# Seven-product FFN, first sweep: who rounds the weights, where raw weights land, and how the operands of the last token group are built

## Chip, core and metric

One core of a Trainium2 chip runs the whole program. The metric is the device time of one execution in microseconds (us); the median of three executions stands for a kernel.

## What is computed

The reference is a two-layer backbone of a latent generator, in fp32: 1024 latent tokens and 256 context tokens, model width 1024, hidden width 4096. Each layer has four mixers (bidirectional SSD, RG-LRU, global and windowed attention) and then the part that matters here, the MLP:

```python
h = modulate(rms_norm(x, g2), shift, scale)
x = x + gate * (square(relu(h @ w_ffn1)) @ w_ffn2)
```

Layer 0 computes this for latent and context tokens, layer 1 for the latent tokens alone, since only these are returned.

## The kernel before

Every fp32 operand of a matmul is split in two: a rounded part `h` (type fp32r) and the remainder `l = raw - h`. A product is then three matmuls, wh·hh, wh·hl and wl·hh (`mm3`, L141 to L143). For weights this is `wsplit`: for each of two halves a DMA of SyncE's queue brings 128x512 raw values, `split` (L242 to L249) rounds them into `wh` and subtracts into `wl`. The pools hold 3 tiles `wh`, 3 `wl`, 2 `raw`, and 8 work tiles `s` (128x512, made by `self.S`) that all helpers share.

The first matmul of the MLP multiplies 1024x1024 latent values (two groups of 512 tokens, g0 and g1) by `w_ffn1` with a seven-product scheme: in blocks of two by two, seven products of sums of blocks replace eight. Two of the products use the weights as they are and the token group g0 alone; they are done first, in `hidden_first` (L1259 to L1307), which runs while the normalised values of g1 are not there yet. The other five, in `hidden_rest`, need sums of operand blocks and sums of weight blocks.

- `hidden_first` steps over the 32 blocks `fc` of 128 hidden rows. For an even `fc`, `part` makes a product of 12 matmuls over the upper half of the contraction; ScalarE copies it out (`copy_a`, L130, b<-qk or b<-pm) and its DMA saves it (L1292); `second` adds the lower half on the same PSUM tile, and `squared` (L1253 to L1256) makes relu and square on ScalarE. In layer 0 every `fc` also has `context`, 24 matmuls over 256 tokens; in layer 1 only the 16 even `fc` are visited, and `second` of a step comes behind `part` of the next one.
- Woven in between (`weave` in `ffn`) stands the work on g1: squares and sums of the RMS norm (`norm_stats`, L412 to L422; its sum over partitions is the tiny matmul L418, its power -0.5 runs on GpSimd, L422), and then `quarter` (L1212 to L1250). This builds, for 4 pairs of rows (k, k+4), the sums of operand blocks on VectorE: `row` makes one modulated row (L136, which reads PSUM, and L1229), then come six subtractions and additions (L1238 to L1243) and five times a rounding CAST and a subtraction (L1248, L1249). It takes two values of k at a time: four rows first, then the 32 operations of both.
- `hidden_rest` begins with `weights(0)`, sums of raw blocks on VectorE (L1345 to L1348), rounding on ScalarE (L130, wh<-s) and subtractions on VectorE (L1351).

While `hidden_first` runs, `act_evicts` is set, and `split` rounds with `gpsimd.tensor_copy` (L246, a CAST); the subtraction is `gpsimd.tensor_sub` (L249). At all other times ScalarE does the rounding.

Each engine works off its own queue in order. The program's framework puts the instructions into these queues, by its own estimate of when each can start, and lets a tile be reused when its last reader is done. So an edit to one helper also shifts the order in which other instructions stand.

Of the kernel before, what the change touches and what calls it, by code (L numbers as in the profile page):

```python
# [13 lines left out]
P = 128  # L14
# [26 lines left out]
def f(ap):  # L41
    return ap.bitcast(F32)


def drain(g):
    for _ in g:
        pass
# [46 lines left out]
class Net:  # L94
# [147 lines left out]

    def split(self, h, l, raw):

        if self.act_evicts:
            self.nc.gpsimd.tensor_copy(h, raw)  # L246
        else:
            self.copy_a(h, raw)
        self.nc.gpsimd.tensor_sub(l, raw, f(h))  # L249


    act_evicts = False

    def wsplit(self, loads, n, new=None):

        if new:
            wl, wh = new(F32R)[:, :n], new(F32R)[:, :n]
        else:
            wl = self.W()[:, :n]
            wh = self.wp.tile([P, 4 * WU], F32R, tag="wh", name="wh", bufs=3)[:, :n]  # L260
        for i in range(2):
            raw = self.R(n // 2)
            for dst, src in loads(raw, i):
                self.nc.sync.dma_start(dst, src)
            c = slice(i * n // 2, (i + 1) * n // 2)
            self.split(wh[:, c], wl[:, c], raw)
        return wh, wl

    def wcols(self, w, c0):

        return self.wsplit(lambda r, i: [(r.rearrange("p (k c) -> p k c", k=4),
                                          w[512 * i:512 * i + 512, c0:c0 + P].rearrange("(k p) c -> p k c", p=P))], 1024)

    def wrows(self, w, r0, new=None):
        return self.wsplit(lambda r, i: [(r, w[r0:r0 + P, 512 * i:512 * i + 512])], 1024, new)
# [937 lines left out]
    def quarter(self, h, t, x, l, t0, rs):  # L1213

        nc = self.nc
        p = self.L[l]
        n = 512
        (hh, hl), (th, tl) = h, t  # L1220
        g0, g1 = G_LAT[0][0], G_LAT[1][0]
        rb = self.PS("pt")
        for j in range(4):
            nc.tensor.transpose(rb[:, j * P:(j + 1) * P], rs[:, j:j + 1].to_broadcast([P, P]), self.ident)

        def row(k):
            a = self.S(n)
            self.stt(a, x.at(k, t0, n), p["s"][1][:, k, 0:1], rb, ALU.mult, ALU.mult)
            nc.vector.tensor_scalar(a, a, p["mods"][:, 24 + k, 0:1], None, op0=ALU.add)  # L1229
            return a  # L1230
        for k2 in range(0, 4, 2):
            rows = [(k, row(k), row(k + 4)) for k in (k2, k2 + 1)]
            yield 2.0
            for k, b12, b22 in rows:
                t1, t2, t3, t4 = (self.S(n) for _ in range(4))
                b11h, b11l, b21h, b21l = (f(r.at(c, g0, n)) for c in (k, k + 4) for r in (hh, hl))
                sub, add = nc.vector.tensor_sub, nc.vector.tensor_add
                sub(t1, b12, b11h)  # L1238
                sub(t3, b22, b12)
                sub(t1, t1, b11l)  # L1240
                sub(t2, b22, t1)
                sub(t4, b21h, t2)
                add(t4, t4, b21l)  # L1243
                yield 2.0
                for raw, r, c, tg in ((t3, t, k + 4, g0), (b22, h, k + 4, g1), (t1, h, k, g1), (t2, t, k, g0),
                                      (t4, t, k, g1)):
                    oh, ol = r[0].at(c, tg, n), r[1].at(c, tg, n)
                    nc.vector.tensor_copy(oh, raw)  # L1248
                    sub(ol, raw, f(oh))  # L1249
                    yield 1.0  # L1250

    def squared(self, r, fc, t0, n, raw=None):

# [4 lines left out]
    def hidden_first(self, l, h, groups):  # L1258


        nc = self.nc
        hh, hl = h
        w1 = self.I["w_ffn1"][l]
        tags = ("pm", "qk", "qk")

        def part(ps, w, t0, n, ks):
            for k in ks:
                c = slice(k * P, k * P + P)
                self.mm3(ps, w[0][:, c], w[1][:, c], hh.at(k, t0, n), hl.at(k, t0, n), k == 0, k in (3, KD - 1), True)
                if k % 2:  # L1270
                    yield n * 2 * 3 * 216e-3 / 512

        def context(fc, w):
            t0, n = G_CTX
            ps = self.PS(self.pick(tags))[:, :n]
            yield from part(ps, w, t0, n, range(KD))
            self.squared(self.B(n), fc, t0, n, ps)

        def second(fc, w, ps):
            t0, n = G_LAT[0]  # L1280
            yield from part(ps, w, t0, n, range(4, KD))
            self.squared(self.B(), fc, t0, n, ps)
        last = None
        for fc in range(0, FFN // P, 1 if len(groups) == 3 else 2):
            w = self.next_weights()[0] if self.wq or self.ready else self.wcols(w1, fc * P)
            if fc % 2 == 0:
                t0, n = G_LAT[0]
                ps = self.PS(self.pick(tags))
                yield from part(ps, w, t0, n, range(4))
                r = self.B()  # L1290
                self.copy_a(r, ps)
                nc.scalar.dma_start(self.part[fc // 2], r)  # L1292

                if len(groups) == 3:
                    yield from context(fc, w)
                    yield from second(fc, w, ps)
                else:
                    if last:
                        yield from second(*last)
                    last = fc, w, ps  # L1300
            else:
                yield from context(fc, w)
        if last:
            yield from second(*last)

    def hidden_rest(self, l, h, t):
# [4 lines left out]
        nc = self.nc  # L1311
        (hh, hl), (th, tl) = h, t
        w1 = self.I["w_ffn1"][l]
        g0, g1 = G_LAT[0][0], G_LAT[1][0]
        n = 512
        NQ = FFN // 256

        def weights(q):
            if q:
                raws = []  # L1320
                for j in range(2):
                    r = self.U()[:, :1024].rearrange("p (k c) -> p k c", k=4)
                    nc.sync.dma_start(r, w1[512 * j:512 * j + 512, 256 * q:256 * q + 256].rearrange("(k p) c -> p k c", p=P))
                    raws.append(r)
                su = [self.U(), self.U()]
                sr = [su[i // 2][:, 512 * (i % 2):512 * (i % 2) + 512] for i in range(4)]
            else:

                raws = {}
                for i, j in ((0, 1), (1, 1), (0, 0), (1, 0)):  # L1330
                    r = (self.S() if j else self.R(512)).rearrange("p (k c) -> p k c", k=4)
                    nc.sync.dma_start(r, w1[512 * j:512 * j + 512, i * P:i * P + P].rearrange("(k p) c -> p k c", p=P))
                    raws[i, j] = r
                sr = [self.S() for _ in range(4)]

            def a(i, j):
                return raws[j][:, :, i * P:i * P + P] if q else raws[i, j]
            wl = [self.W()[:, :1024], self.W()[:, :1024]]
            wh = [self.wp.tile([P, 4 * WU], F32R, tag="wh", name="wh", bufs=3)[:, :1024] for _ in range(2)]
            lo, hi = ([y[i // 2][:, 512 * (i % 2):512 * (i % 2) + 512] for i in range(4)] for y in (wl, wh))  # L1340
            lo.append(self.S(n, F32R))
            hi.append(self.S(n, F32R))
            v = [x.rearrange("p (k c) -> p k c", k=4) for x in sr]
            s1, s2, s3, s4 = 1, 0, 2, 3
            nc.vector.tensor_add(v[s1], a(1, 0), a(1, 1))  # L1345
            nc.vector.tensor_sub(v[s2], v[s1], a(0, 0))
            nc.vector.tensor_sub(v[s3], a(0, 0), a(1, 0))
            nc.vector.tensor_sub(v[s4], a(0, 1), v[s2])  # L1348
            for i in range(4):
                self.copy_a(hi[i], sr[i])  # L1350
                nc.vector.tensor_sub(lo[i], sr[i], f(hi[i]))  # L1351
            h4 = hi[4].rearrange("p (k c) -> p k c", k=4)
            self.copy_a(h4, a(1, 1))
            nc.vector.tensor_sub(lo[4].rearrange("p (k c) -> p k c", k=4), a(1, 1), f(h4))
            return [(hi[i], lo[i]) for i in (s2, s1, s3, 4, s4)]

# [48 lines left out]
    def ffn(self, l, h, t, x_out, groups, pending, tail):  # L1405
# [2 lines left out]
        NF = FFN // P  # L1408
        self.hid = [self.spill() for _ in range(NF)]
        self.part = [self.dp.tile([P, 512], F32, tag=f"r{l}_{q}", name=f"r{l}_{q}") for q in range(NF // 2)]  # L1410
        self.act_evicts = True
        weave((pending, 30), (self.hidden_first(l, h, groups), 90 * len(groups) - 90))
        self.act_evicts = False
        drain(self.hidden_rest(l, h, t))
        x = self.x = self.unspill_x(x_out, T if len(groups) == 3 else 1024)

# [256 lines left out]
```

## Time and profile before

| | |
|---|---|
| median of three runs | 3176.05 us (3173.03 to 3182.01) |
| the profiled execution | 3178.89 us, its span 3177.1 us |
| granted TensorE clock, mean | 0.981 |
| TensorE busy | 95% |
| VectorE, ScalarE, GpSimd busy | 69%, 47%, 27% |

The time is that of the whole program; the span is the part of it in which instructions ran. Layer 0's first sweep lies at about 850 to 1062 us of the span, layer 1's at about 2450 to 2576 us. In the rows PE is TensorE, DVE VectorE, ACT ScalarE, POOL GpSimd; L-numbers are lines of the kernel; idle time stands with what ended it.

### The profile page before, as it was taken

How to read it: one execution, taken by the hardware profiler on the slowest of the kernel's cores; microseconds unless marked ns; L12 is line 12 of the kernel's file. 1: busy time of each engine (PE TensorE's matmuls, PEld its weight loads, DVE VectorE, ACT ScalarE, POOL GpSimd, SP SyncE). 2: the span in 40 equal slices, each digit the busy share in tenths (PEclk: the TensorE clock that was granted, in tenths of full speed). 3: DMA queues.
4: the chain of work that ended last, by engine and by line, in shares of the span. 5: the costliest groups of instructions: out<-in, count | busy, mean ns of one | idle time of the engine just before them, and what ended most of it. 6: DMA issues, size and time to landing. Idle time of an engine off the chain costs nothing.

```text
span 3177.1 us, 45882 instructions
## 1 busy us (share of the span) xinstructions
PE 3006.2 (95%) x16354; PEld 2485.1 (78%) x16354; DVE 2200.5 (69%) x4407; ACT 1490.0 (47%) x3520; POOL 869.3 (27%) x800
## 2 busy tenths in 40 slices
PE   6998999989989899999999999999899889999999
PEld 4688887778778788788888688887777768878887
DVE  5787777877670466667777777778887756667775
ACT  5575776666422344321112576676674334441211
POOL 2214123242576100222112413123334610032220
PEclk8999998999999999999999999999999999999999
DMA  8300012331335545642222410113313454552321
GB/s 316 89 18 24 19 36 80 107 116 47 120 122 159 180 140 179 224 147 83 79 83 89 132 24 15 27 39 101 120 61 113 136 169 153 166 182 90 106 82 59
DMA packets 241941, 335.97 MB, mean 106 GB/s; under 512 B 37424, under 2 KB 159408, under 8 KB 241712
## 3 DMA queue, kind: packets, MB, share of 16 engines
q1 hardware_dynamic: 214064, 286.88, 28.3%
q10 hardware_dynamic: 27648, 46.15, 3.9%
q8 instruction: 129, 2.11, 0.3%
q14 instruction: 100, 0.82, 0.1%
HBM read 253.28 MB, written 79.69 MB: 105 GB/s over the span
## 4 chain that ended last, share of the span: by engine, by line
PE 63%; DVE 11%; DMA 7%; ACT 6%; POOL 6%; issue 5%; SPq 0%; ACTq 0%; POOLq 0%; DVEq 0%
PE pm L143 7%; PE pm L141 7%; PE pm L142 7%; PE qk L142 6%; PE qk L141 6%; PE qk L143 6%; DMA raw<-in_w_ffn 3%; PE pt L142 3%; PE pt L141 3%; PE pt L143 3%; PE pt L752 3%; DVE u L136 3%; POOL wl L249 2%; PE po L761 2%; DMA u<-in_w_ffn 2%
## 5 line engine op out<-in xcount | busy, mean ns | idle before, releaser
L249 POOL TENSOR_TENSOR wl<-raw,wh 128x512 fp32r<-128x512 f32 (+1 forms) x268 | 378.9, 1427 | 1216.5 <-ACT wh L130 899.6
L141 PE MATMUL pm<-u,wh 128*128 128x512 f32 (+1 forms) x1270 | 476.1, 375 | 11.8 <-POOL wh L246 7.3
L143 PE MATMUL pm<-u,wl 128*128 128x512 f32 (+1 forms) x1270 | 469.4, 370 | 13.9 <-POOL wl L249 13.8
L142 PE MATMUL pm<-u,wh 128*128 128x512 f32 (+1 forms) x1270 | 467.9, 369 | 0.0
L141 PE MATMUL qk<-u,wh 128*128 128x512 f32 (+1 forms) x876 | 328.8, 376 | 12.4 <-ACT b L130 10.8
L143 PE MATMUL qk<-u,wl 128*128 128x512 f32 (+1 forms) x876 | 330.6, 377 | 9.4 <-POOL wl L249 9.2
L130 ACT ACTIVATE wh<-raw 128x512 fp32r<-128x512 f32 (+1 forms) x176 | 106.1, 628 | 447.4 <-PE qk L142 177.8
L142 PE MATMUL qk<-u,wh 128*128 128x512 f32 (+1 forms) x812 | 303.8, 374 | 7.1 <-POOL u L443 6.6
L130 ACT ACTIVATE s<-pt 128x512 fp32r<-128x512 f32 (+4 forms) x548 | 251.5, 467 | 120.7 <-PE pt L752 75.0
L141 PEld LDWEIGHTS pm<-u,wh 128*128 128x128 f32 x1270 | 244.5, 193 | 49.5 <-POOL wh L246 7.7
L143 PEld LDWEIGHTS pm<-u,wl 128*128 128x128 f32 x1270 | 243.8, 192 | 49.6 <-POOL wl L249 16.2
L136 DVE SCALAR_TENSOR_TENSOR u<-pm,mods,u 128x512 f32<-128x512 f32 (+1 forms) x312 | 215.6, 692 | 91.2 <-PE pm L143 90.1
L142 PEld LDWEIGHTS pm<-u,wh 128*128 128x128 f32 x1270 | 244.3, 193 | 31.0
L136 DVE SCALAR_TENSOR_TENSOR u<-qk,mods,u 128x512 f32<-128x512 f32 (+1 forms) x296 | 204.8, 692 | 85.9 <-PE qk L143 85.3
L133 ACT ACTIVATE b<-b 128x512 f32<-128x512 f32 (+4 forms) x256 | 146.4, 572 | 149.1 <-DVE b L1375 114.8
L133 ACT ACTIVATE e<-qk,t 128x512 f32<-128x512 f32 (+2 forms) x336 | 188.5, 572 | 42.3 <-DVE t L685 27.2
L143 PEld LDWEIGHTS qk<-u,wl 128*128 128x128 f32 x876 | 166.5, 190 | 45.8 <-POOL wl L249 15.7
L141 PEld LDWEIGHTS qk<-u,wh 128*128 128x128 f32 x876 | 167.0, 191 | 44.8 <-ACT b L130 11.7
L756 DVE TENSOR_TENSOR s<-pt,s 128x512 fp32r<-128x512 f32 (+1 forms) x256 | 166.6, 660 | 40.6 <-ACT s L130 36.4
L1425 DVE TENSOR_TENSOR u<-e,u 128x256 fp32r<-128x256 f32 (+1 forms) x160 | 159.1, 1011 | 46.1 <-ACT u L130 23.8
L142 PEld LDWEIGHTS qk<-u,wh 128*128 128x128 f32 x812 | 154.8, 191 | 36.8 <-POOL u L443 8.5
L141 PE MATMUL pm<-wh,u 128*128 128x256 f32 (+1 forms) x592 | 176.8, 299 | 2.0 <-ACT b L133 1.7
(340 smaller groups left out, 7574.1 us busy)
## 6 DMA issues: line engine op xcount, KB each, us to landing
raw<-in_w_ffn SPq DMA_DIRECT2D x228, 256.0 KB, 2.9
e<-in_w_mod SPq DMA_DIRECT2D x64, 512.0 KB, 4.6
u<-in_w_ffn SPq DMA_DIRECT2D x60, 512.0 KB, 5.0
m<-b ACTq DMA_DIRECT2D x96, 256.0 KB, 2.0
e<-m SPq DMA_DIRECT2D x32, 640.0 KB, 4.3
u<-in_w_mod SPq DMA_DIRECT2D x32, 512.0 KB, 6.9
e<-m SPq DMA_DIRECT2D x32, 512.0 KB, 4.1
xd<-u SPq DMA_DIRECT2D x24, 640.0 KB, 3.3
```

The source lines that it names most:

```text
L130: return self.nc.scalar.activation(o, i, AF.Copy, **k)
L133: self.nc.scalar.activation(o, i, fn, **k)
L136: self.nc.vector.scalar_tensor_tensor(o, a, s, b, op0=op0, op1=op1)
L141: mm(o, ah, bh, start=start, stop=False, skip_group_check=part)
L142: mm(o, ah, bl, start=False, stop=False, skip_group_check=part)
L143: mm(o, al, bh, start=False, stop=stop, skip_group_check=part)
L249: self.nc.gpsimd.tensor_sub(l, raw, f(h))
L752: nc.tensor.transpose(pt[:, e * 256 + hd * P:e * 256 + hd * P + P], prs[hd][0][:, (i + e) * P:(i + e) * P + P], self.ident)
L756: nc.vector.tensor_sub(tl, pt[:, :w], f(th))
L761: nc.tensor.matmul(po[:, :256], V[:, kc, :], th[:, c], start=i + e == 0, stop=False)
L1425: self.nc.vector.tensor_sub(al[:, t], raw[:, t], f(ah[:, t]))
```

## The change

`split` always rounds on ScalarE, and the flag goes. In the first sweep the raw halves of every odd step land in work tiles `s` instead of `raw` tiles, so that four halves can be under way. `quarter` takes one k at a time: two rows from PSUM, six sums, ten operations. The roundings of `weights(0)` move from ScalarE to VectorE. Lines below the edits move up by three to six (L249 becomes L246, L418 L413, L422 L417, L1292 L1289).

```diff
     def split(self, h, l, raw):
-        if self.act_evicts:
-            self.nc.gpsimd.tensor_copy(h, raw)
-        else:
-            self.copy_a(h, raw)
+        self.copy_a(h, raw)
         self.nc.gpsimd.tensor_sub(l, raw, f(h))
...
-    def wsplit(self, loads, n, new=None):
+    def wsplit(self, loads, n, new=None, land=None):
...
-            raw = self.R(n // 2)
+            raw = (land or self.R)(n // 2)
...
-        for k2 in range(0, 4, 2):
-            rows = [(k, row(k), row(k + 4)) for k in (k2, k2 + 1)]
+        for k in range(4):
+            b12, b22 = row(k), row(k + 4)
+            yield 1.0
+            t1, t2, t3, t4 = (self.S(n) for _ in range(4))
...
-            w = self.next_weights()[0] if self.wq or self.ready else self.wcols(w1, fc * P)
+            step = fc // (1 if len(groups) == 3 else 2)
+            w = (self.next_weights()[0] if self.wq or self.ready else
+                 self.wcols(w1, fc * P, self.S if step % 2 else None))
...
             for i in range(4):
-                self.copy_a(hi[i], sr[i])
+                (self.copy_a if q else nc.vector.tensor_copy)(hi[i], sr[i])
                 nc.vector.tensor_sub(lo[i], sr[i], f(hi[i]))
             h4 = hi[4].rearrange("p (k c) -> p k c", k=4)
-            self.copy_a(h4, a(1, 1))
+            (self.copy_a if q else nc.vector.tensor_copy)(h4, a(1, 1))
...
-        self.act_evicts = True
         weave((pending, 30), (self.hidden_first(l, h, groups), 90 * len(groups) - 90))
-        self.act_evicts = False
```

The order of the queues moves with it. ScalarE's queue at the end of layer 0's first sweep, before: `wh_12026` is the rounding of `weights(0)`, `b_11889<-qk_11876` the copy of the partial product of fc 30.

```order
L133 ACTIVATE b_11862<-pm_11837 128x256
L133 ACTIVATE b_11862<-b_11862 128x256
L1256 DMA m49_10082<-b_11862 128x256
L130 ACTIVATE wh_12026<-s_12021 128x512
L130 ACTIVATE b_11889<-qk_11876 128x512
L130 ACTIVATE wh_12026<-s_12020 128x512
L1292 DMA r0_15_10100<-b_11889 128x512
```

The same place in the changed kernel: `wh_11938` is the rounding of the weights of fc 31, `b_11887<-qk_11874` the copy of fc 30's partial product.

```order
L130 ACTIVATE wh_11938<-s_11939 128x512
L133 ACTIVATE b_11817<-qk_11760 128x512
L130 ACTIVATE wh_11938<-s_11943 128x512
L133 ACTIVATE b_11817<-b_11817 128x512
L1250 DMA m48_10081<-b_11817 128x512
L133 ACTIVATE b_11860<-pm_11831 128x256
L133 ACTIVATE b_11860<-b_11860 128x256
L1250 DMA m49_10082<-b_11860 128x256
L130 ACTIVATE b_11887<-qk_11874 128x512
L1289 DMA r0_15_10100<-b_11887 128x512
```

The rounding of `weights(0)` has left the queue; what stands ahead of the copy is the rounding for the step after it.

TensorE's queue in layer 0, around the tiny matmul of g1's norm (`s_10109` holds the summed squares), before: it stands inside `context` of fc 5 (weights `wh_10414`).

```order
L142 MATMUL pm_10423<-u_9882,wh_10414 128x256
L143 MATMUL pm_10423<-u_9881,wl_10413 128x256
L418 MATMUL pt_10442<-one_81,s_10109 128x1 x4
L141 MATMUL pm_10423<-u_9896,wh_10414 128x256
L142 MATMUL pm_10423<-u_9897,wh_10414 128x256
```

In the changed kernel it stands right behind `second` of fc 2 (`qk_10229`) and ahead of `context` of fc 3 (weights `wh_10300`).

```order
L142 MATMUL qk_10229<-u_9861,wh_10220 128x512
L143 MATMUL qk_10229<-u_9860,wl_10219 128x512
L413 MATMUL pt_10442<-one_81,s_10109 128x1 x4
L141 MATMUL pm_10309<-u_9833,wh_10300 128x256
L142 MATMUL pm_10309<-u_9834,wh_10300 128x256
```

It has moved 90 matmuls forward. GpSimd's queue at its three sums of squares, before (`wh_10339` and `wh_10414` are weights of fc 4 and 5):

```order
L412 TENSOR_TENSOR s_10110<-s_10110,s_10200 128x512
L246 CAST wh_10339<-raw_10344 128x512
L249 TENSOR_TENSOR wl_10338<-raw_10344,wh_10339 128x512
L412 TENSOR_TENSOR s_10110<-s_10110,s_10273 128x512
L246 CAST wh_10414<-raw_10415 128x512
L246 CAST wh_10414<-raw_10419 128x512
L412 TENSOR_TENSOR s_10110<-s_10110,s_10355 128x512
```

In the changed kernel the sums (now L407) stand together, and the power (L417) stands between the remainders of fc 3:

```order
L407 TENSOR_TENSOR s_10110<-s_10110,s_10200 128x512
L407 TENSOR_TENSOR s_10110<-s_10110,s_10273 128x512
L407 TENSOR_TENSOR s_10110<-s_10110,s_10355 128x512
L246 TENSOR_TENSOR wl_10299<-raw_10301,wh_10300 128x512
L417 TENSOR_TENSOR t_10449<-t_10447,mhalf_83 128x4
L246 TENSOR_TENSOR wl_10299<-raw_10305,wh_10300 128x512
```

The CASTs are gone, and the sums have moved ahead of the weights of fc 3 to 5.

TensorE's queue in layer 1 around the same matmul, before; 18 matmuls stand between it and the transposes of `quarter` (L1224):

```order
L142 MATMUL qk_26148<-u_25980,wh_26139 128x512
L143 MATMUL qk_26148<-u_25979,wl_26138 128x512
L418 MATMUL pt_26210<-one_81,s_26064 128x1 x4
L141 MATMUL qk_26148<-u_25998,wh_26139 128x512
L142 MATMUL qk_26148<-u_25999,wh_26139 128x512
```

In the changed kernel, where the lines are L413 and L1219, none does.

```order
L142 MATMUL qk_26148<-u_25999,wh_26139 128x512
L143 MATMUL qk_26148<-u_25998,wl_26138 128x512
L413 MATMUL pt_26210<-one_81,s_26064 128x1 x4
L1219 MATMUL pt_26261<-rnd_75,t_26217 128x128 x4
L141 MATMUL qk_26197<-u_25941,wh_26188 128x512
L142 MATMUL qk_26197<-u_25942,wh_26188 128x512
```

The second of them waits for the power on GpSimd, which needs the result of the first.

## Rows read from the trace of the kernel before

**Rows 1.** The page, part 1: busy time, share of the span and instructions of each engine.

```profile
PE 3006.2 (95%) x16354; PEld 2485.1 (78%) x16354; DVE 2200.5 (69%) x4407; ACT 1490.0 (47%) x3520; POOL 869.3 (27%) x800
```

**Rows 2.** ScalarE's copies, layer 1 steps 3, 4, 6, 7, 14: start, us, instruction.

```profile
2476.33 0.60 ACT L130 ACTIVATE b<-qk 128x512 f32<-128x512 f32 x1 [2.21 <-PE qk L143]
...
2490.69 0.60 ACT L130 ACTIVATE b<-pm 128x512 f32<-128x512 f32 x1 [2.63 <-PE pm L143]
...
2502.32 0.60 ACT L130 ACTIVATE b<-qk 128x512 f32<-128x512 f32 x1 [1.54 <-PE qk L143]
2507.90 0.60 ACT L130 ACTIVATE b<-pm 128x512 f32<-128x512 f32 x1 [1.52 <-PE pm L143]
...
2563.95 0.60 ACT L130 ACTIVATE b<-qk 128x512 f32<-128x512 f32 x1 [1.53 <-PE qk L143]
```

**Rows 3.** The same copies in layer 0, fc 4 and fc 28.

```profile
880.09 0.60 ACT L130 ACTIVATE b<-qk 128x512 f32<-128x512 f32 x1 [1.96 <-PE qk L143]
...
1039.39 0.60 ACT L130 ACTIVATE b<-qk 128x512 f32<-128x512 f32 x1 [2.78 <-PE qk L143]
```

**Rows 4.** TensorE by line and form, 900 to 950 us: busy, mean ns, idle before.

```profile
L143 PE MATMUL pm<-u,wl 128*128 128x256 f32 x25 | 8.2, 327 | 12.4 <-POOL wl L249 12.3
```

**Rows 5.** GpSimd in order of time, layer 0: start, us, instruction.

```profile
905.09 15.80 POOL L246 CAST wh<-raw 128x512 fp32r<-128x512 f32 x1 [1.53 <-DMA raw<-in_w_ffn]
```

**Rows 6.** Line L246 alone: count, ns min/median/max; then what GpSimd waited for (us, times).

```profile
L246 POOL CAST wh<-raw x92: 601/616/15797, 820.9 to 2565.0; 128x512 fp32r<-128x512 f32 x92
...
  DMA raw<-in_w_ffn: 83.2, 57
```

**Rows 7.** VectorE in order of time, the end of the same stretch.

```profile
919.99 0.41 DVE L1248 CAST u<-s 128x512 fp32r<-128x512 f32 x1
920.33 0.73 DVE L136 SCALAR_TENSOR_TENSOR s<-u,ms,pt 128x512 f32<-128x512 f32 x1
```

**Rows 8.** Stretches: us, busy (count) of PE, PEld, DVE, ACT, POOL; clock, DMA, GB/s.

```profile
910.00:920.00 10.00, 0.00 (x0) 0.00 (x0) 10.00 (x21) 0.85 (x2) 10.00 (x1) 0.60 0.07 26
1060.00:1070.00 10.00, 7.80 (x39) 6.81 (x40) 5.78 (x9) 5.30 (x11) 0.00 (x0) 0.72 0.44 139
```

**Rows 9.** TensorE by line, layer 1's sweep (2460 to 2600 us).

```profile
L141 PE MATMUL qk<-u,wh 128*128 128x512 f32 x96 | 40.4, 422 | 4.4 <-ACT b L130 3.7 <-DVE b L1371 0.7
...
L141 PE MATMUL pm<-u,wh 128*128 128x512 f32 x45 | 19.6, 436 | 7.3 <-POOL wh L246 7.3
L418 PE MATMUL pt<-one,s 128*128 128x1 f32 x8 | 1.8, 351 | 4.5 <-DVE s L414 4.5
```

**Rows 10.** GpSimd in order of time, layer 1, while `quarter` runs.

```profile
2501.93 3.15 POOL L249 TENSOR_TENSOR wl<-raw,wh 128x512 fp32r<-128x512 f32 x2
...
2547.73 5.40 POOL L246 CAST wh<-raw 128x512 fp32r<-128x512 f32 x2 [6.36 <-DMA raw<-in_w_ffn]
```

**Rows 11.** ScalarE and TensorE in order of time, end of layer 0's sweep.

```profile
1061.03 0.63 ACT L130 ACTIVATE wh<-s 128x512 fp32r<-128x512 f32 x1 [12.31 <-DVE s L1345]
1061.57 0.58 ACT L130 ACTIVATE b<-qk 128x512 f32<-128x512 f32 x1
...
1062.20 0.80 PE L141 MATMUL qk<-u,wh 128*128 128x512 f32 x1 [7.16 <-ACT b L130]
```

**Rows 12.** Norm of g1, engine by engine in order of time (layer 0, then layer 1).

```profile
875.40 0.60 ACT L133 ACTIVATE b<-qk 128x512 f32<-128x512 f32 x1 [2.00 <-PE qk L143]
...
879.54 1.29 POOL L412 TENSOR_TENSOR s<-s 128x512 f32<-128x512 f32 x1
...
2481.41 0.69 DVE L414 TENSOR_TENSOR s<-s 128x512 f32<-128x512 f32 x1 [9.30 <-POOL s L412]
...
2484.27 1.02 POOL L422 TENSOR_TENSOR t<-t,mhalf 128x4 f32<-128x4 f32 x1 [2.90 <-DVE t L420]
```

**Rows 13.** VectorE while `quarter` runs in layer 1: us, busy (count), clock, DMA, GB/s.

```profile
2491.13:2552.10 60.97, 60.96 (x80) 0.96 0.48 151
```

**Rows 14.** DMA issues of the page: KB each, median us from issue to landing.

```profile
raw<-in_w_ffn SPq DMA_DIRECT2D x228, 256.0 KB, 2.9
```

More of the change, by code (lines that the diff above doesn't have):

```diff
@@ L243, in split @@
     def split(self, h, l, raw):
-        if self.act_evicts:
-            self.nc.gpsimd.tensor_copy(h, raw)
-        else:
-            self.copy_a(h, raw)
+        self.copy_a(h, raw)
         self.nc.gpsimd.tensor_sub(l, raw, f(h))
-    act_evicts = False
-    def wsplit(self, loads, n, new=None):
+    def wsplit(self, loads, n, new=None, land=None):
         if new:
@@ L267, in wsplit, with wcols @@
         return wh, wl
-    def wcols(self, w, c0):
+    def wcols(self, w, c0, land=None):
         return self.wsplit(lambda r, i: [(r.rearrange("p (k c) -> p k c", k=4),
-                                          w[512 * i:512 * i + 512, c0:c0 + P].rearrange("(k p) c -> p k c", p=P))], 1024)
+                                          w[512 * i:512 * i + 512, c0:c0 + P].rearrange("(k p) c -> p k c", p=P))], 1024,
+                           land=land)
     def wrows(self, w, r0, new=None):
@@ L1230, in row @@
             return a
-        for k2 in range(0, 4, 2):
-            rows = [(k, row(k), row(k + 4)) for k in (k2, k2 + 1)]
-            yield 2.0
[L1234 to L1250, printed above, removed]
+        for k in range(4):
+            b12, b22 = row(k), row(k + 4)
+            yield 1.0
+            t1, t2, t3, t4 = (self.S(n) for _ in range(4))
+            b11h, b11l, b21h, b21l = (f(r.at(c, g0, n)) for c in (k, k + 4) for r in (hh, hl))
+            sub, add = nc.vector.tensor_sub, nc.vector.tensor_add
+            sub(t1, b12, b11h)
+            sub(t3, b22, b12)
+            sub(t1, t1, b11l)
+            sub(t2, b22, t1)
+            sub(t4, b21h, t2)
+            add(t4, t4, b21l)
+            yield 2.0
+            for raw, r, c, tg in ((t3, t, k + 4, g0), (b22, h, k + 4, g1), (t1, h, k, g1), (t2, t, k, g0),
+                                  (t4, t, k, g1)):
+                oh, ol = r[0].at(c, tg, n), r[1].at(c, tg, n)
+                nc.vector.tensor_copy(oh, raw)
+                sub(ol, raw, f(oh))
+                yield 1.0
     def squared(self, r, fc, t0, n, raw=None):
```

## The prediction

> **What bounds the kernel now.** I read the totals of the page first: TensorE is busy for 95% of the span [rows 1]. The change touches only the two first sweeps, so it can win only where TensorE stands still or runs at a lower clock inside them. To see where that is, I took ScalarE in order of time and used the copies of finished partial products as mile posts, since each even fc has one.
>
> In layer 1 the quickest step, from 2502.32 to 2507.90, takes 5.58 us [rows 2]. That is 24 matmuls of 512 columns with no gap, TensorE's own pace. A pair of steps in layer 0 has the columns of 48 such matmuls, so 11.16 us. Against this:
>
> - Layer 0: from fc 4 to fc 28, 880.09 to 1039.39, are 12 pairs in 159.3 us [rows 3]. At TensorE's pace they would take 12 × 11.16 = 133.9. **25.4 us** are lost.
> - Layer 1: from step 3 to step 14, 2476.33 to 2563.95, are 11 steps in 87.6 us [rows 2]. At 5.58 they would take 61.4. **26.2 us** are lost.
>
> Then I looked for what TensorE waited for. In layer 0 one wait of 12.3 us stands out, for a remainder wl from GpSimd [rows 4]. Behind it is one rounding CAST that took 15.80 us [rows 5], where the middle one takes 0.62 [rows 6]. It lasted while VectorE worked off `quarter` without a break, and ended when VectorE came to an operation that reads PSUM, at 920.33 [rows 7]. TensorE did nothing from 910 to 920, VectorE 21 operations, and the granted clock fell to a mean of 0.60 [rows 8]. The rest of the loss is spread over the pairs, and there the reader sees GpSimd idle until a raw half has landed, 83.2 us in 57 places over both layers [rows 6]: with two raw tiles a load starts only when an earlier remainder is done.
>
> In layer 1 TensorE waits 4.5 us for the sum of squares [rows 9], in a step of 14.36 us instead of 5.58 (2476.33 to 2490.69) [rows 2], so 8.8 are lost with the slow matmuls behind the wait; and 7.3 us for a CAST [rows 9], which with another took 5.40 us after 6.36 idle for its raw half [rows 10].
>
> At the end of each sweep stands one more wait. In layer 0 ScalarE's queue has the rounding of `weights(0)`, wh<-s, ahead of the copy b<-qk. The rounding waited 12.31 us for VectorE, the copy waited with it, and TensorE lost 7.16 us [rows 11]. In layer 1 the same copy cost 3.7 us [rows 9].
>
> What a wait costs beyond itself is read from the stretch behind that of layer 0, 1060 to 1070: TensorE worked for 7.80 us at a mean clock of 0.72 [rows 8]. With half speed, 1.2 of 2.4 GHz, as the lower level, 5.6 us of the 10 were slow, 2.2 of them idle, so 3.4 us of work ran at half speed: 1.7 us lost, my estimate for each long wait.
>
> **The change, part by part.**
>
> *Roundings to ScalarE.* 92 CASTs of 0.62 us leave GpSimd [rows 6], 57 us, and come to ScalarE, where one takes 0.63 [rows 11]: 58 us more on an engine busy 47% [rows 1]. A rounding can only delay what stands behind it, the copies and squares. In the order it stands one to two steps ahead of the matmuls that need it (fc 31's ahead of fc 30's copy), so I cost it at nothing; the cover is that lead, and without it two roundings, 1.25 us a step, are the price (rival 3). The two stuck CASTs go. Gain: 12.3 + 1.7 = **14.0** in layer 0, 7.3 + 1.7 = **9.0** in layer 1.
>
> *Four raw halves.* What is left of the losses is 25.4 − 14.0 = 11.4 in layer 0 and 26.2 − 9.0 − 8.8 = 8.4 in layer 1, mostly late raw halves. Bounds: all of it, 19.8, or nothing, if VectorE and GpSimd slow each other as before. I take **14**, since the idle time that names the raw half, 83.2 us, is far above it.
>
> *End of the sweep.* The roundings of `weights(0)` leave ScalarE's queue and take VectorE 5 × 0.41 us [rows 7], when it has nothing else. Gain 7.16 + 3.7 + 2 × 1.7 = **14.3**. What is late next is the raw data of `weights(1)`, at the same distance from its use as before; I cost that at nothing, and at 4 us at most.
>
> *The norm of g1, moved.* In layer 0 its matmul stands 90 matmuls earlier. TensorE reaches it when `second` of fc 2 ends, which is where ScalarE's relu starts, at 875.40 [rows 12]. The last square now stands behind that relu and its square on ScalarE: three times 0.6 us, then GpSimd's sum 1.29 and VectorE's 0.69 [rows 12], so 3.8 us in which TensorE stands. Behind it fc 3's second remainder stands after the power, 1.02 us [rows 12]: about 1.5 more. With 1.7 for slow matmuls I take **7 lost**; bounds 2, if the square comes early, and 11. In layer 1 the sum comes sooner, as GpSimd has no CASTs between its parts, but nothing stands between the norm's matmul and the transposes that need the power: TensorE waits there for some 0.2 + 1.02 us, and then 1.3 for a remainder. With slow matmuls I keep 4 of the 8.8: gain **4.8**.
>
> *`quarter` row by row.* The same operations, but VectorE comes to one that reads PSUM after some 16 operations instead of 32, and its rows now share tiles `s` with raw halves. Undisturbed it did 21 operations in 10 us [rows 8], so 16 take 7.6. If one remainder per layer is held up that long, layer 0 has about 8 us to spare by the order, layer 1 only 3.6 (5.58 to the next use, less a rounding and a subtraction): 7.6 − 3.6 + 1.7, about **6 lost**. Bounds: 0, and rival 2. Here the rows stand against a rule. In the rows two remainders took 3.15 us together while VectorE was just as dense [rows 10], not much over two free ones, so they got through between its operations. The Trainium skill says in "SBUF — State Buffer", section "Who interferes with whom", that a VectorE instruction with two SBUF inputs contends with a GpSimd instruction that reads SBUF, and that whoever comes first holds the shared ports for the whole instruction. By that rule a subtraction is shut out like a rounding, and the sum would be that of rival 2. The trace agrees for one CAST of 15.80 us, and not for these two remainders.
>
> **Sum.** 14.0 + 9.0 + 14 + 14.3 + 4.8 − 7 − 6 = 43.1 us gained. The profiled execution took 3178.89, 2.8 more than the median, so by its own time the sum is 3135.8; from the median of 3176.05 it is **3133**, my forecast.
>
> **Rivals.**
>
> *2. The remainders get stuck in the CASTs' place.* For it: the long hold lasted as long as VectorE's operations on SBUF did [rows 5, 7], and these are as many as before. Against: the two remainders of 3.15 us [rows 10]. Then the 14.0 and 9.0 are not won, and the 6 above are part of that loss: 43.1 − 23.0 + 6 = 26 us gained, **3150**. It is what the rule quoted above would give.
>
> *3. ScalarE becomes the late one.* If raw halves land so late that the lead of the roundings is gone, a step waits for its two roundings, 1.25 us: 60 us over 48 steps. For it: copies and roundings share one queue, and one such order cost 7.16 us [rows 11]. Against: the lead. With two thirds of the steps hit, 40 us are given back: no change, **3173**.
>
> *4. Slower: the tiles `s`.* SyncE's queue now has loads that wait until a row of `quarter` frees its tiles, with the loads of other steps behind them. A row has 20 operations; 80 took 60.96 us in layer 1 [rows 13], so 15.2 a row beside GpSimd. Load 2.9 [rows 14], rounding 0.63 and remainder 1.3 on top make 20.0, where three steps of layer 1 give 16.7. If a row holds the load that is needed next, TensorE loses 3.3 + 1.7 = 5 us, 40 for 8 rows, and the 14 for raw halves are not won: 43.1 − 54 = −11, **3187**. It decides above a row of 12 us, and if the load it holds is the next one; in the order it is mostly two to six steps ahead.
>
> **How the numbers follow.** Forecast 0.66, rival 2 0.16, rival 3 0.10, rival 4 0.08. The forecast's own range runs from a gain of 58 (no remainder held, all of the raw halves, little lost at the norm) to one of 30: 3118 to 3146. The whole range takes in rival 2: 3118 to 3158. A difference under 0.3%, 9.5 us, can't be told from no change here. Forecast and rival 2 are faster, 0.82; rival 3 is the same but for 0.01, so 0.09; slower with rival 4, 0.09.
>
> **What would show it.** Right: no CAST on GpSimd in the sweeps; pairs of layer 0 at 11.2 to 11.5 us, steps of layer 1 at 5.6; no wait for b from L130 at the sweeps' ends; ScalarE's busy time up by some 55 us, GpSimd's down by 75; a new wait of about 4 us for the sum of squares (L409) near 875 us. Rival 2 shows in remainders of 5 us and more and in TensorE's waits for wl; rival 3 in waits for wh from ScalarE at many steps; rival 4 in ScalarE idle for raw halves in s, and SyncE waiting on VectorE. The forecast is wrong if the two sweeps together are not at least 20 us shorter.

## The result, and the profile after

The change made the kernel faster: 3124.51 us median of four runs (3116.95 to 3126.26) against 3174.54 (3166.93 to 3182.01) in the same comparison, a ratio of 0.9827 with a 95% interval of 0.9803 to 0.9851. The forecast was 3133, with 3118 to 3158 as its range.

The profiled execution has a span of 3123.5 us, 53.6 less than before. To see in which stage they went, I cut both traces at four marks: the power of the norm ahead of each sweep (GpSimd, L422, now L417; in layer 0 that of the context tokens), and VectorE's first sum of `hidden_rest` (L1371, now L1368).

| us | before | after | difference |
|---|---|---|---|
| start to the first mark | 830.6 | 830.2 | -0.4 |
| layer 0, start and sweep | 243.4 | 217.1 | **-26.3** |
| between the sweeps | 1373.2 | 1374.4 | +1.2 |
| layer 1, start and sweep | 139.6 | 110.8 | **-28.8** |
| the rest | 590.2 | 591.1 | +0.9 |

So all of it lies in the two sweeps. The page's part 1, after:

```profile
PE 2992.9 (96%) x16354; PEld 2477.7 (79%) x16354; DVE 2203.9 (71%) x4417; ACT 1527.6 (49%) x3602; POOL 797.9 (26%) x708
```

Against [rows 1] GpSimd lost 92 instructions and 71 us, ScalarE gained 82 instructions and 38 us, VectorE the ten roundings of `weights(0)`. Stretches of layer 0's sweep after, with the columns of [rows 8]:

```profile
850.00:870.00 20.00, 19.64 (x108) 16.54 (x107) 11.92 (x15) 16.84 (x32) 10.03 (x9) 0.95 0.42 143
870.00:890.00 20.00, 14.94 (x81) 13.55 (x80) 3.07 (x3) 8.93 (x18) 13.37 (x11) 0.83 0.44 130
890.00:1040.00 150.00, 149.65 (x953) 135.15 (x952) 61.70 (x92) 68.36 (x142) 73.47 (x50) 1.00 0.53 164
```

From 890 us on TensorE stands still for 0.35 us in 150, at full clock. Nothing is left to win in that part; before, there was the hole of 910 to 920 us and a loss in nearly every pair. The only stretch that is not full is 870 to 890. ScalarE's copies of partial products after, layer 0 (fc 4, 20, 22, 28 and 30), then layer 1 (steps 3, 6, 7 and 14):

```profile
887.36 0.58 ACT L130 ACTIVATE b<-qk 128x512 f32<-128x512 f32 x1
...
977.58 0.60 ACT L130 ACTIVATE b<-qk 128x512 f32<-128x512 f32 x1 [1.12 <-PE qk L143]
988.86 0.60 ACT L130 ACTIVATE b<-qk 128x512 f32<-128x512 f32 x1 [1.14 <-PE qk L143]
...
1022.71 0.60 ACT L130 ACTIVATE b<-qk 128x512 f32<-128x512 f32 x1 [1.14 <-PE qk L143]
1034.02 0.60 ACT L130 ACTIVATE b<-qk 128x512 f32<-128x512 f32 x1 [1.97 <-PE qk L143]
...
2453.61 0.60 ACT L130 ACTIVATE b<-qk 128x512 f32<-128x512 f32 x1 [6.36 <-PE qk L143]
...
2472.52 0.60 ACT L130 ACTIVATE b<-qk 128x512 f32<-128x512 f32 x1 [0.85 <-PE qk L143]
2478.10 0.60 ACT L130 ACTIVATE b<-pm 128x512 f32<-128x512 f32 x1 [0.81 <-PE pm L143]
...
2517.25 0.60 ACT L130 ACTIVATE b<-qk 128x512 f32<-128x512 f32 x1 [0.81 <-PE qk L143]
```

Pairs take 11.28 us and steps 5.58, TensorE's own pace or close to it, up to the last copy, which now waits for TensorE alone; in [rows 11] it stood behind a rounding. Between the copies that the prediction used as mile posts layer 0 now takes 135.4 us, against 159.3 before and 133.9 at that pace, and layer 1 63.6, against 87.6 and 61.4.

Where TensorE still waits in layer 0 is the norm of g1, moved forward. Its rows, engine by engine:

```profile
871.71 0.60 ACT L133 ACTIVATE b<-qk 128x512 f32<-128x512 f32 x1 [1.00 <-PE qk L143]
...
872.87 0.61 ACT L133 ACTIVATE s<-u 128x512 f32<-128x512 f32 x1
...
873.62 1.26 POOL L407 TENSOR_TENSOR s<-s 128x512 f32<-128x512 f32 x1 [2.57 <-ACT s L133]
...
874.92 1.75 DVE L409 TENSOR_TENSOR s<-s 128x512 f32<-128x512 f32 x1 [3.32 <-POOL s L407]
...
876.73 1.87 PE L413 MATMUL pt<-one,s 128*128 128x1 f32 x8 [5.06 <-DVE s L409]
```

The last square stands behind relu and square of `second`, and GpSimd, VectorE and TensorE follow one after the other: 5.06 us of standstill where before there was next to none. In layer 1 TensorE's largest waits in the sweep are 1.8 for a remainder, 1.5 for a rounding and 1.4 for the power, where [rows 9] has 4.5, 7.3 and 3.7, 15.5 together.

One thing was not expected to be harmless. The remainders of the halves that land in s, by line and form (count, then least, median and most ns):

```profile
L246 POOL TENSOR_TENSOR wl<-s,wh x44: 1271/1296/7495, 874.9 to 2516.2; 128x512 fp32r<-128x512 f32 x44
```

and GpSimd in order of time in layer 0 (start, duration, of two instructions):

```profile
1017.60 8.75 POOL L246 TENSOR_TENSOR wl<-s,wh 128x512 fp32r<-128x512 f32 x2 [5.30 <-ACT wh L130]
```

A subtraction was held for 7.5 us while VectorE worked off a row. TensorE did not wait for it, as the stretch to 1040 shows.

### The profile page after: what moved, and what is told of

It is laid out like the page before. It is cut to its first block, busy times and chain, and to the rows that moved or that the text cites. A ratio compares the mean times of both kernels' runs of the same rounds, so it can differ in the third digit from the quotient of the medians.

```text
span 3123.5 us, 45937 instructions
## 1 busy us (share of the span) xinstructions
PE 2992.9 (96%) x16354; PEld 2477.7 (79%) x16354; DVE 2203.9 (71%) x4417; ACT 1527.6 (49%) x3602; POOL 797.9 (26%) x708
## 3 DMA queue, kind: packets, MB, share of 16 engines
q1 hardware_dynamic: 214064, 286.88, 28.8%
## 4 chain that ended last, share of the span: by engine, by line
PE 61%; DVE 5%; ACT 4%; DMA 2%; issue 2%; POOL 2%; ACTq 0%; SPq 0%; POOLq 0%; DVEq 0%
PE qk L143 8%; PE qk L142 8%; PE qk L141 8%; PE pm L143 7%; PE pm L141 6%; PE pm L142 6%; PE pt L142 3%; PE pt L143 3%; PE pt L141 3%; DVE u L136 1%; PE pt L747 1%; PE po L756 1%; PE po L757 1%; POOL wl L246 1%; ACT s L130 1%
## 5 line engine op out<-in xcount | busy, mean ns | idle before, releaser
L246 POOL TENSOR_TENSOR wl<-raw,wh 128x512 fp32r<-128x512 f32 (+1 forms) x224 | 317.7, 1432 | 1229.5 <-ACT wh L130 1130.3
L130 ACT ACTIVATE wh<-raw 128x512 fp32r<-128x512 f32 (+1 forms) x224 | 135.7, 628 | 476.6 <-PE qk L142 165.4
L136 DVE SCALAR_TENSOR_TENSOR u<-pm,mods,u 128x512 f32<-128x512 f32 (+1 forms) x312 | 215.5, 692 | 91.1 <-PE pm L143 90.0
L141 PEld LDWEIGHTS pm<-u,wh 128*128 128x128 f32 x1270 | 243.4, 192 | 41.3 <-DVE u L136 4.3
L136 DVE SCALAR_TENSOR_TENSOR u<-qk,mods,u 128x512 f32<-128x512 f32 (+1 forms) x296 | 204.8, 692 | 84.5 <-PE qk L143 83.6
```

What stands on the lines that cost most here:

```text
L130: return self.nc.scalar.activation(o, i, AF.Copy, **k)
L136: self.nc.vector.scalar_tensor_tensor(o, a, s, b, op0=op0, op1=op1)
L141: mm(o, ah, bh, start=start, stop=False, skip_group_check=part)
```

## The experiments

All ratios are to the kernel before, on the chip of the same batch, with 95% intervals; the change itself is 0.9827. Four experiments undo one part of it, four do one or two parts alone, four change something beside it.

**1. Two raw tiles again.**

```diff
-                 self.wcols(w1, fc * P, self.S if step % 2 else None))
+                 self.wcols(w1, fc * P))
```

> The changed kernel, but every raw half of the first sweep lands in the two raw tiles again. Theory (the loads of raw halves cost TensorE up to 19.8 us, and four tiles won them back): about 3145 us, 15 to 22 above the changed kernel, and GpSimd or ScalarE idle until a raw half has landed in every pair of steps; pairs of layer 0 at 11.7 to 12 us. Rival (only the CASTs on GpSimd mattered, since rounding on ScalarE starts earlier anyway): 3125 to 3130, pairs at 11.3.

Measured 3178.08 us, 0.9991 (0.9966 to 1.0016). Both expectations fell: the whole gain is gone, by the ratios some 52 us, not 20. TensorE by line, in layer 0 the copies and in layer 1 the remainders that it waits for:

```profile
L141 PE MATMUL qk<-u,wh 128*128 128x512 f32 (+1 forms) x260 | 92.0, 356 | 21.2 <-ACT b L130 21.0
...
L143 PE MATMUL qk<-u,wl 128*128 128x512 f32 x100 | 42.1, 428 | 16.8 <-POOL wl L246 16.8
```

GpSimd and ScalarE in order of time, layer 0:

```profile
903.79 9.79 POOL L246 TENSOR_TENSOR wl<-raw,wh 128x512 fp32r<-128x512 f32 x2 [1.58 <-ACT wh L130]
...
915.38 0.63 ACT L130 ACTIVATE wh<-raw 128x512 fp32r<-128x512 f32 x1 [7.50 <-DMA raw<-in_w_ffn]
916.72 0.63 ACT L130 ACTIVATE wh<-raw 128x512 fp32r<-128x512 f32 x1 [0.40 <-DMA raw<-in_w_ffn]
917.25 0.58 ACT L130 ACTIVATE b<-qk 128x512 f32<-128x512 f32 x1
```

GpSimd was held at a remainder, so its raw tile came free late, so the next half landed late; ScalarE's rounding waited 7.5 us for it, and the copy of a finished partial product stood behind that rounding. TensorE waited 21.0 us in layer 0 for such copies. The price is rival 3's, a rounding that waits for its raw half with a copy behind it; what starts it is rival 2's, a remainder that is held. In layer 1 it is rival 2 alone, 16.8 us for remainders. In the changed kernel TensorE waits for no copy in layer 0 for longer than 0.3 us.

**2. Two values of k at a time.** The loop of `quarter` as before the change.

```diff
-        for k in range(4):
-            b12, b22 = row(k), row(k + 4)
+        for k2 in range(0, 4, 2):
+            rows = [(k, row(k), row(k + 4)) for k in (k2, k2 + 1)]
...
```

> The changed kernel, but quarter takes two values of k at a time again, four rows from PSUM and then 32 operations on SBUF. Theory (the hold needs a CAST on GpSimd): no change within 5 us, 3120 to 3130; at most one remainder held for 8 to 16 us, which the lead of the weights covers in layer 0 and not in layer 1. Rival (the hold depends on how long VectorE works without reading PSUM, whatever GpSimd does): remainders of up to 16 us and TensorE waiting for wl, 3140 to 3148.

Measured 3124.97 us, 0.983 (0.9812 to 0.9847): no difference, as the theory had it. The longest remainder took 4.7 us. With four halves under way the shape of `quarter` is worth nothing that can be measured.

**3. weights(0) on ScalarE.**

```diff
-                (self.copy_a if q else nc.vector.tensor_copy)(hi[i], sr[i])
+                self.copy_a(hi[i], sr[i])
...
-            (self.copy_a if q else nc.vector.tensor_copy)(h4, a(1, 1))
+            self.copy_a(h4, a(1, 1))
```

> The changed kernel, but the roundings of weights(0) are on ScalarE again, where they stand in the queue ahead of the copy of fc 30. Theory as predicted (the queue order makes TensorE wait): the 14 us come back, 3138. Rival (with four raw halves under way the raw data of weights(0) has landed about 28 us earlier in relation to the sweep, so the rounding does not wait and the queue order is harmless): 3125 to 3128.

Measured 3132.3 us, 0.9851 (0.983 to 0.9871), about 8 us over the change, between the two. The intervals of the two ratios overlap; but experiment 2, on the same chip and level with the change, ran at 3123 to 3127 us, and this one at 3131 to 3133. ScalarE and TensorE at the end of layer 0:

```profile
1035.06 0.63 ACT L130 ACTIVATE s<-s 128x512 fp32r<-128x512 f32 x1 [8.32 <-DVE s L1345]
...
1038.99 0.62 ACT L130 ACTIVATE wh<-s 128x512 fp32r<-128x512 f32 x1
...
1040.37 0.60 ACT L130 ACTIVATE b<-qk 128x512 f32<-128x512 f32 x1 [0.46 <-ACT b L133]
...
1041.02 0.79 PE L141 MATMUL qk<-u,wh 128*128 128x512 f32 x1 [3.85 <-ACT b L130]
```

VectorE's sums are ready 2 us before TensorE has finished the product, but ScalarE has waited for them, and five roundings with squares between them still stand ahead of the copy: 3.85 us for TensorE in place of 7.16.

**4. Roundings on GpSimd.** `split` with the flag as before, all else as in the change.

```diff
-        self.copy_a(h, raw)
+        if self.act_evicts:
+            self.nc.gpsimd.tensor_copy(h, raw)
+        else:
+            self.copy_a(h, raw)
...
+        self.act_evicts = True
         weave((pending, 30), (self.hidden_first(l, h, groups), 90 * len(groups) - 90))
+        self.act_evicts = False
```

> The changed kernel, but the roundings of the first sweep are on GpSimd again; raw halves, rows and weights(0) as in the change. Theory (CASTs on GpSimd get stuck while VectorE is dense): one or two CASTs of 5 us or more, TensorE waits for wl, 3135 to 3148 less some 6 us, as the norm's matmul of layer 0 stands in its old place and costs nothing there. Rival (four raw halves and shorter rows were all that counted): 3118 to 3125.

Measured 3134.75 us, 0.9858 (0.984 to 0.9877), 10 us over the change and 44 under the kernel before on the same chip. This lies in the theory's range, but the stuck CAST is not what it paid for. In layer 0 it lost nothing: the sweep took 216.5 us by the marks above, against 217.1. One CAST of a half in s was held for 7.66 us there, and it didn't matter. Layer 1, where no rounding or remainder took 5 us, lost: 124.3 against 110.8. Line L246 over the whole span:

```profile
L246 POOL CAST wh<-s x44: 611/743/7662, 870.5 to 2525.4; 128x512 fp32r<-128x512 f32 x44
```

and TensorE's largest wait by line in layer 1:

```profile
L141 PE MATMUL qk<-u,wh 128*128 128x512 f32 x100 | 42.0, 422 | 5.5 <-POOL wh L246 4.9 <-DVE b L1373 0.6
```

**5. The kernel before, with roundings on ScalarE.**

```diff
-        self.act_evicts = True
         weave((pending, 30), (self.hidden_first(l, h, groups), 90 * len(groups) - 90))
```

> The kernel before with one part of the change: the roundings of the first sweep on ScalarE. Theory (stuck CASTs cost 23 us, the norm's matmul moved forward costs some 5): 3155 to 3160, and the losses to raw halves and at the sweeps' ends stay. Rival (GpSimd's remainders get stuck instead): 3172 to 3180, remainders of 5 us and more.

Measured 3184.98 us, 1.003 (1.0015 to 1.0046): slower. The rival was right, and beyond it. GpSimd in order of time in layer 1:

```profile
2484.24 15.95 POOL L249 TENSOR_TENSOR wl<-raw,wh 128x512 fp32r<-128x512 f32 x2 [3.31 <-ACT wh L130]
2505.48 16.47 POOL L249 TENSOR_TENSOR wl<-raw,wh 128x512 fp32r<-128x512 f32 x2 [5.29 <-ACT wh L130]
```

and TensorE by line there:

```profile
L143 PE MATMUL qk<-u,wl 128*128 128x512 f32 x100 | 41.3, 420 | 26.9 <-POOL wl L249 26.8
```

Twice two subtractions took 16 us instead of 2.6, and TensorE waited 26.8 us for them. So it is not the CAST that gets stuck but whatever GpSimd does then. In layer 0 TensorE waited another 18.0 us for copies behind roundings, as in experiment 1.

**6. The kernel before, with weights(0) on VectorE.** The edit of experiment 3 the other way round.

```diff
-                self.copy_a(hi[i], sr[i])
+                (self.copy_a if q else nc.vector.tensor_copy)(hi[i], sr[i])
...
-            self.copy_a(h4, a(1, 1))
+            (self.copy_a if q else nc.vector.tensor_copy)(h4, a(1, 1))
```

> The kernel before with one part of the change: the roundings of weights(0) on VectorE. Theory (queue order on ScalarE costs 14 us over both layers): 3160, with no wait of TensorE for a copy by L130 at the ends of the sweeps. Rival (TensorE then waits for the weights themselves, whose raw data lands late): 3168 to 3175, and a wait for wh or wl of hidden_rest in place of the other.

Measured 3178.78 us, 0.9999 (0.9976 to 1.0021): nothing. The rival holds in its mechanism. ScalarE's copy, VectorE and TensorE at the end of layer 0:

```profile
1055.21 0.60 ACT L130 ACTIVATE b<-qk 128x512 f32<-128x512 f32 x1 [3.87 <-PE qk L143]
...
1063.51 0.69 DVE L1345 TENSOR_TENSOR s<-raw,s 128x512 f32<-128x512 f32 x1 [107.81 <-DMA raw<-in_w_ffn]
...
1066.53 0.50 PE L141 MATMUL qk<-u,wh 128*128 128x512 f32 x1 [2.88 <-DVE wh L1350]
```

Counted from the first mark the copy comes 5 us earlier than in [rows 11], and then TensorE waits for the weights themselves, whose raw halves have only just landed, 8.3 us behind the copy. In the changed kernel the same sum starts at 1031.88, 2.1 us ahead of the copy.

**7 and 8. Where the norm's matmul stands.** The share of the interleaved work decides; in 7 it is 24 in both layers, in 8 it is 24 in layer 0 and 36 in layer 1.

```diff
-        weave((pending, 30), (self.hidden_first(l, h, groups), 90 * len(groups) - 90))
+        weave((pending, 24), (self.hidden_first(l, h, groups), 90 * len(groups) - 90))
```

> The changed kernel with the share of the interleaved work on the last token group set from 30 to 24, which in the order moves the norm's matmul of layer 0 behind the partial product of a later block. Theory (the new wait of 5.06 us there, with slow matmuls about 7, is the price of the order): 3116 to 3119, and no wait at L413 in layer 0. Rival (the quarter then ends later and hidden_rest waits for it): 3125 or slower.

Measured 3133.52 us, 0.9865 (0.9832 to 0.9899), a miss for the theory; the time is the rival's, its reason is not. TensorE's wait for the sum of squares of g1 is gone in layer 0, and the sweep there became longer, 223.9 us against 217.1, since TensorE now waits for remainders during the quarter. TensorE by line in layer 0:

```profile
L143 PE MATMUL pm<-u,wl 128*128 128x256 f32 (+1 forms) x140 | 42.7, 305 | 9.5 <-POOL wl L246 9.5
```

Nearly all of that is one wait. ScalarE, GpSimd and TensorE in order of time:

```profile
908.31 0.63 ACT L130 ACTIVATE wh<-s 128x512 fp32r<-128x512 f32 x1 [0.46 <-ACT b L133]
...
909.01 9.09 POOL L246 TENSOR_TENSOR wl<-s,wh 128x512 fp32r<-128x512 f32 x1 [13.93 <-ACT wh L130]
...
918.16 0.58 PE L143 MATMUL pm<-u,wl 128*128 128x256 f32 x1 [8.66 <-POOL wl L246]
```

The rounding stood in ScalarE's queue behind a square and waited for no load, and GpSimd had been idle for 13.93 us until it came. So the lead was gone, and of a hold of 9.09 us TensorE paid 8.66, with four halves under way. So the 5.06 us are a price of the order, but what takes their place may cost more.

In experiment 8:

```diff
-        weave((pending, 30), (self.hidden_first(l, h, groups), 90 * len(groups) - 90))
+        weave((pending, 24 if len(groups) == 3 else 36), (self.hidden_first(l, h, groups), 90 * len(groups) - 90))
```

> As the one before in layer 0, and 36 in layer 1, where the norm's matmul then stands 11 matmuls earlier and 6 matmuls stand between it and the transposes. Theory: layer 1's 1.4 us wait for the power goes, but the sum of squares may be late: within 4 us of the one before. Rival: the earlier place makes TensorE wait for the sum of squares as it did in layer 0, 5 to 7 us slower than the one before.

Measured 3126.63 us, 0.9849 (0.9818 to 0.988): 7 us under experiment 7, against both expectations in size, but the intervals of the two overlap; layer 1's sweep took 108.2 us, against 114.4 there and 110.8 in the change.

**9 and 10. Landing alone, and landing with ScalarE.** The kernel before with the parameter `land` of the change; in 10 also without the flag.

```diff
-            w = self.next_weights()[0] if self.wq or self.ready else self.wcols(w1, fc * P)
+            step = fc // (1 if len(groups) == 3 else 2)
+            w = (self.next_weights()[0] if self.wq or self.ready else
+                 self.wcols(w1, fc * P, self.S if step % 2 else None))
```

> The kernel before with one part of the change: the raw halves of odd steps of the first sweep land in tiles s; roundings stay on GpSimd, weights(0) on ScalarE, two values of k at a time. Theory by now (undoing this part cost all of the gain, undoing the roundings' engine 10 us, undoing weights(0) 8): four raw halves alone carry most of the gain, 3140 to 3150, with sweep 1 longer than in the changed kernel and a wait for a copy by L130 at the sweeps' ends. Rival (the gain exists only with roundings on ScalarE and four halves together): 3165 or more.

Measured 3140.23 us, 0.9866 (0.985 to 0.9881). One part, some 43 us. Layer 0's sweep takes 217.0 us, as in the change; layer 1's 128.0. Line L246 and what it waited for:

```profile
L246 POOL CAST wh<-raw x48: 602/620/1163, 818.5 to 2520.1; 128x512 fp32r<-128x512 f32 x48
L246 POOL CAST wh<-s x44: 604/632/3117, 868.6 to 2525.3; 128x512 fp32r<-128x512 f32 x44
  DMA raw<-in_w_ffn: 17.6, 4
  DMA s<-in_w_ffn: 11.6, 3
```

GpSimd's idle time until a half has landed fell from the 83.2 us of [rows 6] to 29.2, with the CASTs still on it.

> The kernel before with two parts: raw halves of odd steps in tiles s, and roundings on ScalarE. With the kernel before, the one with ScalarE alone and the one with landing alone this makes the four corners. Theory (ScalarE's roundings cost time with two raw halves and gain some 10 us with four; the other two parts give at most the 8 of weights(0)): 3128 to 3135. Rival (rows one at a time are needed when tiles s are shared): 3145 or more.

Measured 3130.24 us, 0.9828 (0.9809 to 0.9846). That closes a square:

| ratio to before | roundings on GpSimd | roundings on ScalarE |
|---|---|---|
| two halves under way | 1 | 1.003 |
| four halves under way | 0.9866 | 0.9828 |

The edit of the roundings' engine costs 0.3% at the top and wins 0.4% at the bottom.

The run also bears on experiment 3, since it leaves the roundings of `weights(0)` on ScalarE too, but has two values of k at a time. ScalarE at the end of layer 0:

```profile
1030.99 0.63 ACT L130 ACTIVATE s<-s 128x512 fp32r<-128x512 f32 x1 [3.89 <-DVE s L1351]
...
1036.30 0.60 ACT L130 ACTIVATE b<-qk 128x512 f32<-128x512 f32 x1 [0.46 <-ACT b L133]
```

The same instructions stand ahead of the copy as in experiment 3, but they begin 5 us sooner, counted from the first mark, and TensorE waits for no copy there. Experiment 3 has a hold of 7.50 us at 1017.95, as the change has; here no remainder of that sweep took over 3.2 us, and the raw tiles for `weights(0)`, which come free when remainders are done, came free sooner. So the 8 us of experiment 3 are not a fixed worth of the edit: by the ratio this run, without the edit, is level with the change, though its sweep of layer 1 is longer, 115.5 us against 110.8.

**11. Four raw tiles and six tiles s**, so that nothing is shared.

```diff
-        self.sp = en(tc.tile_pool(name="sp", bufs=8))
+        self.sp = en(tc.tile_pool(name="sp", bufs=6))
...
-        return self.wp.tile([P, 2 * WU], F32, tag="raw", name="raw", bufs=2)[:, :n]
+        return self.wp.tile([P, 2 * WU], F32, tag="raw", name="raw", bufs=4)[:, :n]
...
-                 self.wcols(w1, fc * P, self.S if step % 2 else None))
+                 self.wcols(w1, fc * P))
```

> The changed kernel, with four raw tiles and six tiles s in place of two and eight, so that raw halves and quarter do not share; the same memory in all. Theory (what counts is how many halves are under way, not where): within 6 us of the changed kernel, 3119 to 3131. Rival (six tiles are too few for quarter and the norm, which then run late, and hidden_rest or the norm's matmul waits): 3135 or more.

Measured 3137.13 us, 0.9854 (0.9839 to 0.987). By the total this is the rival's number, but not its place: the two sweeps take 217.0 and 112.6 us, as in the change, and the stage between them takes 1390.0 instead of 1374.4. In that stage stand the rest of layer 0's MLP and the mixers of layer 1, whose helpers draw on the tiles s as well; which of them misses the two was not traced. For the sweeps only the number of halves counts, not where they land.

**12. Share 30 in layer 0, 36 in layer 1.**

```diff
-        weave((pending, 30), (self.hidden_first(l, h, groups), 90 * len(groups) - 90))
+        weave((pending, 30 if len(groups) == 3 else 36), (self.hidden_first(l, h, groups), 90 * len(groups) - 90))
```

> The changed kernel with the share of the interleaved work set to 36 in layer 1 alone (30 stays in layer 0). Theory (layer 1's norm and transposes no longer stand next to each other; its sweep took 108.2 us instead of 110.8 with this share, layer 0's stays as it is): 2 to 4 us under the changed kernel, 3120 to 3123. Rival (that difference is noise): no change within 2 us.

Measured 3121.85 us, 0.9813 (0.9795 to 0.983). This is the lowest of all, but its interval overlaps that of the change, and its sweep of layer 1 took 111.9 us, not 108.2. It can't be told from the change: inconclusive.

## Why the prediction was right, and where its steps were not

The total was right, 43 us forecast and 50 measured between the medians, for a sum whose terms were in part wrong. What held it was the ceiling of the first point below; that the terms came out near it is luck, since one that was three times too small made up for two that were too large.

- **What bounds it, and how much could be won:** right. By the pace of 5.58 us per step the sweeps had 51.6 us of loss within them and 14.3 at their ends; 55.1 were won in the two stages. The changed kernel runs at that pace but for 3.7 us between the mile posts of both layers, so the ceiling was real. Of the signs that I had named, ScalarE's busy time rose by 38 us and not by 55.
- **Roundings to ScalarE, 14.0 + 9.0:** this is the step that failed. Alone it made the kernel slower by 0.3% (experiment 5), and undone it cost 10 us (experiment 4). I had put the 12.3 us down to the CAST; a subtraction is held just as long, 14.7 to 16.4 us in experiment 5. In layer 1 I booked the whole wait of 7.3 us on the CASTs, though the 6.36 us of [rows 10] before them were a late raw half. And the rounding's lead, which I took from the order as given, needs two things: raw halves that land early, for with two of them TensorE waited 21.0 us for copies behind roundings (experiment 1); and an early place in ScalarE's queue, which experiment 7 has lost in one step.
- **Four raw halves, 14 of at most 19.8:** the term that was far too small. Alone it gave 1.34%, some 43 us (experiment 9); without it nothing is left (experiment 1). My bound of 19.8 held only what was left after the waits that I had booked elsewhere. But a held GpSimd costs TensorE only what the lead of the weights doesn't cover, and the lead is made of raw halves. With four of them holds of 7.5 us in the change and 7.66 in experiment 4 cost TensorE nothing in layer 0. It is no rule: one of 9.09 cost 8.66 in experiment 7.
- **End of the sweep, 14.3:** the wait went, as forecast, but not by this edit alone: 0.9999 in experiment 6, since the raw data was just as late. With four halves the edit is worth 8 us beside a hold (experiment 3), and without one the kernel lost nothing by leaving it out (experiment 10). What I called late next, `weights(1)`, was not; it was `weights(0)` itself.
- **The norm of g1, 7 lost in layer 0, 4.8 won in layer 1:** right in place and about right in size. 5.06 us instead of 3.8 for the standstill, because VectorE's sum took 1.75 us beside GpSimd's subtraction instead of 0.69, and slow matmuls behind it (clock 0.83 in those 20 us). In layer 1 waits of 1.4, 1.8 and 1.5 us stand where I had 2.5.
- **`quarter` row by row, 6 lost:** nothing was lost, and the edit does nothing measurable (experiment 2). The rival of held remainders was right as a mechanism: in experiment 5 subtractions are shut out like roundings. The rule that I quoted from the Trainium skill ("SBUF — State Buffer", "Who interferes with whom") says that the engine that comes first has the shared ports for one whole instruction. The traces agree on who shuts out whom and not on how long: the longest holds lasted through 28 to 33 of VectorE's instructions. I had set the two remainders of [rows 10] against it; they were one of two courses that such a stretch can take, see below.
- **Rivals 3 and 4:** rival 3's price shows in layer 0 of experiments 1 and 5, 21.0 and 18.0 us for copies behind roundings, so what decides it is the number of halves; in layer 1 both paid for held remainders, 16.8 and 26.8. Of rival 4 the first step is there, since SyncE's loads waited for rows of `quarter` for 16 us in layer 0 and 15 in layer 1, but not the price: TensorE doesn't wait for these loads.

What stays open: how the 43 us of the landing tiles divide between two things. With four halves a hold may be covered, as in the change, and long holds were also fewer. In the sweeps of the four profiled executions with two halves (before, experiments 1, 5 and 6) 11 roundings or remainders took 5 us and more, the longest 16.84; in the ten with four halves there were 7, the longest 9.09. Experiment 9 had none, so its gain says nothing of the cover. No run was made that changes one and not the other. It is not chance between executions, though: the same hold comes back in kernels that differ elsewhere, 7.50 us in the change and in experiments 3 and 12 (which ran on two chips), and 9.09 in 7 and 8.

## What to carry to other kernels

Ask first how far ahead the operands of the bound engine are made, and what that lead is made of; here two more landing tiles brought most of the gain. A stall that shows on one instruction (a CAST of 15.80 us) is not cured by moving that instruction, if its engine has others; the lead has to cover it. And terms of a sum read off one trace are not independent: moving work to an in-order queue pays only once nothing in front of it waits for a load, so test the parts in a square, each alone and both together.

## What the runs showed of the hardware that was not expected

GpSimd beside a dense VectorE goes one of two ways in these traces. Either the two take turns, and VectorE's subtractions of 0.68 us take up to 1.79 while GpSimd's take about 1.6; or GpSimd gets nothing until VectorE's run of operations on SBUF ends: 15.80 us for a CAST before, 14.7 to 16.4 for a subtraction in experiment 5, 7.5 in the change. All 18 holds of 5 us and more in the sweeps of these runs ended so: six when VectorE came to L136, which reads PSUM, and twelve at a pause of VectorE, the shortest of 0.03 us.

The same run of some 33 operations of VectorE takes 16.5 to 18.5 us the second way, while GpSimd is held, and 27 to 30 the first way (before and experiments 5 and 6 have both). So it is not the length of the run that decides. What does was not found; that a hold comes back unchanged in other kernels, as said above, points at the order and not at chance.
